# Projecting the first group of heads between the group norms of a two-block transformer kernel

## The chip, the core and the metric

The kernel runs as one program on one core of a Trainium2 chip. The metric is the device time of one execution in microseconds (us), the median of several runs. TensorE (PE) does the matrix products, VectorE (DVE) and ScalarE (ACT) the elementwise work, GpSimd (POOL) some more of it, and SyncE (SP) issues most of the loads. Each engine executes its own list of instructions in a fixed order and waits on semaphores for the others.

## The reference, cut to what matters

Two transformer blocks run one after the other on `x[1, 256, 1024]` in fp32. The change is inside the first block, between its bidirectional RWKV-7 scan and its mixture of experts. For 8 heads of width 64, the two directions of the scan are summed to `y`; then come a group norm per head, a bonus and a gate, and the projection and merge of the two branches:

```python
yn = ((y - mu) * rsqrt(var + GN_EPS)) * ln_g + ln_b          # per head of 64
y_a = (yn + bonus) * g                                        # 256 x 512
merged = sigmoid(gate_a) * (y_a @ proj_a) + sigmoid(gate_b) * (y_b @ proj_b)
x = x + m[2] * (merged @ w_out)                               # then the router and the experts
```

`y_b` is the result of a neighbourhood attention that is done long before. `gate_a` and `gate_b` are 2048 columns of the first input projection `w_in`. The router needs all of the new `x`, so nothing of the experts' work can begin before the last column of `merged @ w_out`.

## The kernel before

Every fp32 product is made of three matmuls in a reduced type (`mm3`, L117 to L121): each operand is a pair of a high and a low part. `split` (L123 to L129) makes such a pair of a 128x512 weight piece: ACT copies the high part (L127) and DVE subtracts it (L128). `prepare` does the same for the large 128x2048 pieces of `w_out` (L180 on ACT, L181 on DVE), and `split_into` for results that are already in PSUM (L940 on ACT, L941 on DVE).

`rwkv` (L876) weaves several generators into one another. Three slots work off the 16 units of the scan (4 chunks of time, 2 directions, 2 groups of four heads). Beside them run `gates` (gate columns of `w_in`, then the products of `proj_b`; their pieces are loaded at L997 and L1015, split by L127/L128, and summed in the PSUM bank "gg"), a generator for the modulation (loads `mr` at L296, worked on by POOL), and `rwkv_out`. `rwkv_out` normalises the sum `y` in four steps `norm(t, g)`: t is a half of the 256 tokens, g a group of four heads. A norm transposes `y` on PE (L898), reduces and squares on DVE and ACT (L903 to L909), takes an inverse square root in some ten small DVE steps (L104 to L115), scales on DVE (L913 to L915), transposes back on PE (L919) and makes the pair `yaT` (L940, L941). The order is group 0, t = 1 and 0, then group 1, t = 1 and 0; each waits until the two units of the scan that it sums are done.

The last unit of the scan ends with L862 to L872 (PE products, with L863, L864, L869 between them), L772 to L784 (PE) and the addition to `y` on DVE (L790). Two units are in hand at once near the end: L828, L834, L837 (PE) with L823 (ACT) and L830 (DVE) belong to the inversion of a triangular matrix in the last one.

After the scan `merge` (L1139) makes `y_a @ proj_a` from eight weight pieces: `product(q, k2)` takes column block q and the head group k2. First the four products of group 0 are issued, then for each q that of group 1, followed by L1173 and L1174 (DVE), L1175 (ACT) and L1176 (DVE), which make the merged pair `mTk`, `mTv`. Then `halves` multiplies by `w_out`, whose four large pieces are split by L180/L181; L1183 and L1184 add the result to the residual. Between them L1737 and L1749 on PE make the router's inputs.

The program's text is not the final order. A scheduler with a cost model reorders the instructions when the kernel is built, subject to the data, the buffers and explicit constraints (`issue_after` keeps an instruction behind another one); after that the order on each engine is fixed. So a norm can stand on DVE between instructions of the scan, and a split of `w_out` between instructions of a norm.

Of the kernel before, what the change touches and what calls it, by code (L numbers as in the profile page):

```python
# [8 lines left out]
F32 = mybir.dt.float32  # L9
# [3 lines left out]
AF = mybir.ActivationFunctionType  # L13
ALU = mybir.AluOpType
# [5 lines left out]
P = 128  # L20
# [51 lines left out]
class Kernel:  # L72
# [803 lines left out]
    def rwkv(self, gates, rest):  # L876
# [5 lines left out]
        turns(gens + [(0, gates), (0, rest), (0, self.rwkv_out(units))])  # L882


    def rwkv_out(self, units):


        nc = self.nc
# [4 lines left out]
        def norm(t, g):  # L893
# [26 lines left out]
            self.split_into(self.yaT[:, 2 * g:2 * g + 2, t * P:(t + 1) * P],  # L920
                            b[:, 0:256].rearrange("p (k t) -> p k t", k=2))
# [66 lines left out]
    def gates(self, pool):  # L988
# [3 lines left out]
        for q in range(8):  # L992
            b = self.bank("gg", 1)
            for k2 in range(4):
# [3 lines left out]
                wt = self.split(pool, raw, [P, 2, 256], "w", bufs=2)  # L998
# [12 lines left out]
        for q in range(4):  # L1011
            b = self.bank("gg", 1)
            for k2 in range(2):
# [3 lines left out]
                wt = self.split(pool, raw, [P, 2, 256], "w", bufs=2)  # L1017
# [6 lines left out]
            nc.vector.scalar_tensor_tensor(g, g, 1.0, b, op0=ALU.add, op1=ALU.mult)  # L1024

# [112 lines left out]

    def merge(self, fp):  # L1139
        nc, a = self.nc, self.a  # L1140
        tt, stt = nc.vector.tensor_tensor, nc.vector.scalar_tensor_tensor
        banks = [self.bank() for _ in range(4)]

        def product(q, k2):

            raw = fp.tile([P, 2, 256], F32, tag="wr", name="wr", bufs=3)
            nc.sync.dma_start(raw, a["proj_a"][0][k2 * 256:(k2 + 1) * 256, 256 * q:256 * q + 256]
                              .rearrange("(k p) n -> p k n", p=P))
            wt = self.split(fp, raw, [P, 2, 256], "w", bufs=2)
            for k in range(2):  # L1150
                for j in range(2):
                    self.mm3(banks[q][:, 256 * j:256 * j + 256], wt[:, k, j * P:(j + 1) * P], self.yaT[:, 2 * k2 + k, :],
                             start=(k2 == k == j == 0), stop=(k2 == 1 and k == 1), skip_group_check=True)
        for q in range(4):
            product(q, 0)
# [40 lines left out]
    def router_inputs(self, pool):  # L1196
        nc = self.nc
# [951 lines left out]
```

## Time and profile before

| | us |
|---|---|
| runs | 1572.23, 1576.36, 1580.75 |
| median | 1576.36 |
| the profiled execution, its own time | 1566.17 |
| its span, from the first to the last instruction | 1564.5 |
| outside the span | 1.7 |
| PE busy in the span | 1457.9 (93%) |

| part of the span | us |
|---|---|
| last addition to `y` (L790) ends | 588.34 |
| last pair `yaT` (L941) ends | 605.83 |
| last column of `merged @ w_out` is taken up (L1183) | 643.40 |

All times in what follows are on the profiled execution's own scale, counted from the start of its span. A row of the timeline reads: start, duration, engine, line and operation, what is written from what, and in brackets how long the engine stood idle before it and what ended that.

### The profile page before, as it was taken

How to read it: one execution, taken by the hardware profiler on the slowest of the kernel's cores; microseconds unless marked ns; L12 is line 12 of the kernel's file. 1: busy time of each engine (PE TensorE's matmuls, PEld its weight loads, DVE VectorE, ACT ScalarE, POOL GpSimd, SP SyncE). 2: the span in 40 equal slices, each digit the busy share in tenths (PEclk: the TensorE clock that was granted, in tenths of full speed). 3: DMA queues.
4: the chain of work that ended last, by engine and by line, in shares of the span. 5: the costliest groups of instructions: out<-in, count | busy, mean ns of one | idle time of the engine just before them, and what ended most of it. 6: DMA issues, size and time to landing. Idle time of an engine off the chain costs nothing.

```text
span 1564.5 us, 26010 instructions
## 1 busy us (share of the span) xinstructions
PE 1457.9 (93%) x10562; PEld 1113.8 (71%) x10562; DVE 889.1 (57%) x1869; ACT 634.8 (41%) x1035; POOL 306.6 (20%) x316
## 2 busy tenths in 40 slices
PE   6899999999999886689999899999999999999996
PEld 3677777778788675543443368699988887998885
DVE  3778458676766676622311255565556755755555
ACT  2433545444454452110110145554444645544443
POOL 1002049765666410490000000000000000000000
PEclk9899999898999897889999999999999999999999
DMA  9511223222232133689999935355554452555542
GB/s 325 162 42 66 68 84 122 79 80 73 69 94 77 56 134 129 258 331 420 421 419 421 380 98 173 108 170 185 186 187 168 155 197 87 183 189 188 188 162 74
DMA packets 118328, 274.21 MB, mean 175 GB/s; under 512 B 8591, under 2 KB 31795, under 8 KB 106935
## 3 DMA queue, kind: packets, MB, share of 16 engines
q1 hardware_dynamic: 115608, 270.13, 49.1%
q10 hardware_dynamic: 2559, 2.32, 0.5%
q8 instruction: 85, 1.39, 0.4%
q14 instruction: 44, 0.36, 0.1%
q0 software_dynamic: 32, 0.00, 0.0%
HBM read 271.36 MB, written 1.06 MB: 174 GB/s over the span
## 4 chain that ended last, share of the span: by engine, by line
PE 54%; DVE 1%; ACT 1%; issue 0%; DVEq 0%; ACTq 0%
PE mm L119 12%; PE mm L120 12%; PE mm L121 12%; PE mm L1476 11%; PE mm L1461 1%; PE mm L1619 1%; PE mm L1540 1%; PE mm L1876 1%; PE mm L1737 1%; PE mm L1895 1%; PE mm L1849 0%; PE mm L1905 0%; PE mm L214 0%; PE mm L1838 0%; DVE wl L181 0%
## 5 line engine op out<-in xcount | busy, mean ns | idle before, releaser
L181 DVE TENSOR_TENSOR wl<-wr,wh 128x2048 fp32r<-128x2048 f32 (+2 forms) x130 | 271.6, 2089 | 208.1 <-ACT wh L180 195.7
L180 ACT ACTIVATE wh<-wr 128x2048 fp32r<-128x2048 f32 (+2 forms) x130 | 227.2, 1749 | 160.7 <-PE mm L121 108.1
L121 PE MATMUL mm<-xTh,wl 128*128 128x256 f32 x512 | 143.9, 281 | 0.0
L120 PE MATMUL mm<-xTl,wh 128*128 128x256 f32 x512 | 143.7, 281 | 0.0
L119 PE MATMUL mm<-xTh,wh 128*128 128x256 f32 x512 | 143.2, 281 | 0.0
L119 PE MATMUL mm<-wh,fh 128*128 128x512 f32 x256 | 101.4, 396 | 0.0
L121 PE MATMUL mm<-wh,fl 128*128 128x512 f32 x256 | 101.1, 395 | 0.0
L120 PE MATMUL mm<-wl,fh 128*128 128x512 f32 x256 | 101.0, 395 | 0.0
L300 POOL TENSOR_SCALAR mr<-mr,silu_c 128x512 f32<-128x512 f32 x56 | 97.8, 1747 | 5.3 <-DMA mr<-in_mod_w_dram 5.1
L120 PEld LDWEIGHTS mm<-xTl,wh 128*128 128x128 f32 x512 | 96.2, 188 | 0.9 <-DVE xTl L941 0.3
L119 PEld LDWEIGHTS mm<-xTh,wh 128*128 128x128 f32 x512 | 96.1, 188 | 0.7
L119 PE MATMUL mm<-wh,xTh 128*128 128x512 f32 (+1 forms) x272 | 95.7, 352 | 0.7 <-ACT big L1813 0.5
L121 PEld LDWEIGHTS mm<-xTh,wl 128*128 128x128 f32 x512 | 96.3, 188 | 0.0
L120 PE MATMUL mm<-wl,xTh 128*128 128x512 f32 (+1 forms) x272 | 93.0, 342 | 0.0
L121 PE MATMUL mm<-wh,xTl 128*128 128x512 f32 (+1 forms) x272 | 92.5, 341 | 0.0
L301 POOL TENSOR_TENSOR mra<-mra,mr 128x512 f32<-128x512 f32 x56 | 74.0, 1322 | 4.2
L823 ACT ACTIVATE nt<-mm 128x512 f16<-128x512 f32 x80 | 47.6, 595 | 59.3 <-PE mm L837 51.8
L119 PEld LDWEIGHTS mm<-wh,xTh 128*128 128x128 f32 x272 | 51.2, 188 | 8.6 <-ACT big L1813 0.7
L121 PEld LDWEIGHTS mm<-wh,fl 128*128 128x128 f32 x256 | 48.1, 188 | 11.5
L120 PEld LDWEIGHTS mm<-wl,fh 128*128 128x128 f32 x256 | 48.1, 188 | 10.7
L119 PEld LDWEIGHTS mm<-wh,fh 128*128 128x128 f32 x256 | 48.1, 188 | 10.6
L121 PEld LDWEIGHTS mm<-wh,xTl 128*128 128x128 f32 x272 | 51.2, 188 | 6.2
(569 smaller groups left out, 3496.4 us busy)
## 6 DMA issues: line engine op xcount, KB each, us to landing
wr<-in_w_up_dram SPq DMA_DIRECT2D x32, 1024.0 KB, 5.6
wr<-in_w_down_dram SPq DMA_DIRECT2D x32, 1024.0 KB, 5.1
wr<-in_w_in_dram SPq DMA_DIRECT2D x22, 1024.0 KB, 5.1
wr<-in_moe_w_dram SPq DMA_DIRECT2D x21, 1024.0 KB, 8.7
wh<-in_moe_w_dram SPq DMA_DIRECT2D x20, 1024.0 KB, 13.8
wl<-in_moe_w_dram SPq DMA_DIRECT2D x20, 1024.0 KB, 12.0
mr<-in_mod_w_dram SPq DMA_DIRECT2D x64, 256.0 KB, 2.8
wx<-in_moe_w_dram SPq DMA_DIRECT2D x14, 1024.0 KB, 10.3
```

The costliest lines, as they stand in the source:

```text
L119: mm(out, l.hi, r.hi, start=start, stop=False, **kw)
L120: mm(out, l.hi, r.lo, start=False, stop=False, **kw)
L121: mm(out, l.lo, r.hi, start=False, stop=stop, **kw)
L180: self.nc.scalar.activation(w.hi, raw, AF.Copy)
L181: self.nc.vector.tensor_tensor(w.lo, raw, w.hi.bitcast(F32), op=ALU.subtract)
L300: nc.gpsimd.tensor_scalar(raw, raw, self.sc[:, k, 0:1], None, op0=ALU.mult)
L301: nc.gpsimd.tensor_tensor(acc, acc, raw, op=ALU.add)
L823: nc.scalar.activation(nt, v4(bz), AF.Copy)
L1461: mm(b[:, k * 256:k * 256 + 256], part[:, t, 2 * q + k, :], sel[:, t].rearrange("p j c -> p (j c)"), start=(i == 0), stop=(i == 3))
L1476: mm(b[r], lT[:, k0 + k, c0 + SLOT * j:c0 + SLOT * j + SLOT], w[:, k], start=(start and k == 0), stop=(stop and k == n - 1))
L1540: mm(acc[2 * n + k // 2][:, k % 2], part[:, k * P:(k + 1) * P], back, start=False, stop=(g == 7 and part is y.lo), skip_group_check=True)
L1619: mm(banks[t], first[:, k, t * P:(t + 1) * P], w[:, k, :], start=(k == 0), stop=False)
```

## The change

1. `rwkv_out` begins only when `gates` has emitted everything ("gates" is added to its first condition and set at the end of `gates`).
2. The products of head group 0 with `proj_a` move out of `merge` and in between the norms: norm(1,0), norm(0,0), three weight pieces, products q = 0 and 1, then product 2 ahead of norm(1,1) and product 3 ahead of norm(0,1). Each product asks for the next weight piece.
3. The split weight pieces of `gates` and of `proj_a` get three buffers instead of two (`bufs=3`).
4. `prepare` of `w_out` is issued behind the last norm's two splitting instructions (`issue_after(self.normed[...])`).
5. The banks are named differently: the router's sums take "gg", `router_inputs` a common bank.

```diff
-        while not {("prep", d, g, i), "bonus"} <= self.past:
+        while not {("prep", d, g, i), "bonus", "gates"} <= self.past:
             yield
+        self.merged = []
         self.yaT = Pair(...)
-        for g in range(2):
-            for t in (1, 0):
-                while not {(0, g, 2 + t), (1, g, 3 - t)} <= self.past:
-                    yield
-                yield from norm(t, g)
+        yield from until((0, 0, 3), (1, 0, 2))
+        yield from norm(1, 0)
+        yield from until((0, 0, 2), (1, 0, 3))
+        yield from norm(0, 0)
+        self.pieces = [self.merge_piece(fp, n) for n in range(3)]
+        for q, tag in enumerate(("gg", "nn1")):
+            self.merge_product(fp, q, 0, tag)
+            yield
+        yield from until((0, 1, 3), (1, 1, 2))
+        self.merge_product(fp, 2, 0, "nn2")
+        yield from norm(1, 1)
+        yield from until((0, 1, 2), (1, 1, 3))
+        self.merge_product(fp, 3, 0, "nn0")
+        yield from norm(0, 1)
...
-                wt = self.split(pool, raw, [P, 2, 256], "w", bufs=2)
+                wt = self.split(pool, raw, [P, 2, 256], "w", bufs=3)
...
+        self.past.add("gates")
...
+    def merge_product(self, fp, q, k2, tag=None):
+        if tag:
+            self.merged.append(self.bank(tag, 1))
+        wt, b = self.pieces.pop(0), self.merged[q]
+        for k in range(2):
+            for j in range(2):
+                self.mm3(b[:, 256 * j:256 * j + 256], wt[:, k, j * P:(j + 1) * P], self.yaT[:, 2 * k2 + k, :],
+                         start=(k2 == k == j == 0), stop=(k2 == 1 and k == 1), skip_group_check=True)
+        n = 4 * k2 + q + 3
+        if n < 8:
+            self.pieces.append(self.merge_piece(fp, n))
...
-        for q in range(4):
-            product(q, 0)
...
         for q in range(4):
-            product(q, 1)
+            self.merge_product(fp, q, 1)
...
-        self.rbank = self.spare()
+        with self.tc.issue_after(self.normed[0]), self.tc.issue_after(self.normed[1]):
+            self.prepare()
+        self.rbank = self.bank("gg", 1)
```

In the changed kernel the lines behind L900 are shifted: the pair `yaT` is made by L921 and L922, the merge's steps are L1196 to L1199, the addition to the residual is L1209 and L1210, the loads of `gates` L1012, its evictions L1020 and L1039.

On DVE, where the scan ends, the rows of before around the last addition to `y` (L790) are these; the small steps are the inverse root of the third norm, and `wl` 128x2048 is a split of `w_out`.

```order
L113 TENSOR_TENSOR rs_t<-rs_u 128x4
L790 TENSOR_TENSOR y_2065<-y_2065,mm 128x256
L114 SCALAR_TENSOR_TENSOR rs_w<-rs_t,va 128x4
L181 TENSOR_TENSOR wl<-wr,wh 128x2048
L115 SCALAR_TENSOR_TENSOR rs_u<-rs_w,rs_u 128x4
L181 TENSOR_TENSOR wl<-wr,wh 128x2048
L113 TENSOR_TENSOR rs_t<-rs_u 128x4
L114 SCALAR_TENSOR_TENSOR rs_w<-rs_t,va 128x4
L115 SCALAR_TENSOR_TENSOR grs<-rs_w,rs_u 128x4
L913 TENSOR_TENSOR yn<-yn,grs 128x256
L181 TENSOR_TENSOR wl<-wr,wh 128x2048
```

In the changed kernel the same place on DVE reads as follows, from the last unit's L864 to the first norm, norm(1,0).

```order
L864 TENSOR_TENSOR rr_7223<-rr_7223,mm 128x512
L128 TENSOR_TENSOR wl<-wr,wh 128x512
L869 TENSOR_TENSOR rq_7476<-rr_7223,mm 128x512
L1039 SCALAR_TENSOR_TENSOR gt<-gt,mm 128x512
L128 TENSOR_TENSOR wl<-wr,wh 128x512
L774 TENSOR_TENSOR z_7887<-mm,krT_7226 128x256
L790 TENSOR_TENSOR y_2065<-y_2065,mm 128x256
L903 TENSOR_REDUCE mu<-mm 128x4
L904 TENSOR_SCALAR mu<-mu 128x4
L905 TENSOR_TENSOR yn<-mm,mu 128x256
```

All four norms now stand behind the last addition to `y`; before, the first two and the beginning of the third stood ahead of it, and three splits of `w_out` stood inside the third.

Further down DVE's list, inside the third norm, norm(1,1), the changed kernel has splits of `proj_a` pieces (`wl` 128x512).

```order
L114 SCALAR_TENSOR_TENSOR rs_w<-rs_t,va 128x4
L128 TENSOR_TENSOR wl<-wr,wh 128x512
L115 SCALAR_TENSOR_TENSOR grs<-rs_w,rs_u 128x4
L913 TENSOR_TENSOR yn<-yn,grs 128x256
L914 TENSOR_TENSOR yn<-yn,gf 128x256
L128 TENSOR_TENSOR wl<-wr,wh 128x512
L915 TENSOR_TENSOR yn<-yn,gf 128x256
L128 TENSOR_TENSOR wl<-wr,wh 128x512
L922 TENSOR_TENSOR yaTa<-mm,yaTw 128x2x128
```

Three of its four splits stand ahead of L915, the norm's last scaling, and the fourth stands ahead of the pair `yaT` (L922).

On PE, the last unit's products of before stand behind the transposes (L919) of the second norm.

```order
L1200 MATMUL mm<-rw,fac 128x16 x8
L919 MATMUL mm<-ident,yn 128x128 x2
L868 MATMUL mm<-z_7913,mk_7392 128x128 x4
L898 MATMUL mm<-ident,y_2066 128x128 x2
L872 MATMUL mm<-rq_7476,tT_2093 128x128 x4
L772 MATMUL mm<-mk_7392,rr_7223 64x128 x4
L781 MATMUL mm<-mk_7392,zv 64x128 x2
```

In the changed kernel L868, the last ten matmuls of `gates` and L872 follow each other (just ahead of these rows), and the first norm's transposes come behind the unit's last product; the 48 matmuls of head group 0 (with `yaTw`, `yaTa`) begin behind the third norm's first transposes.

```order
L772 MATMUL mm<-mk_7392,rr_7223 64x128 x4
L781 MATMUL mm<-mk_7392,zv 64x128 x2
L781 MATMUL mm<-mk_7392,rr_7223 64x128 x2
L781 MATMUL mm<-mk_7392,zv 64x128 x2
L781 MATMUL mm<-mk_7392,rr_7223 64x128 x2
L784 MATMUL mm<-z_7887,sbd_2092 128x128 x2
L898 MATMUL mm<-ident,y_2066 128x128 x2
L919 MATMUL mm<-ident,yn 128x128 x2
L898 MATMUL mm<-ident,y_2065 128x128 x2
L919 MATMUL mm<-ident,yn 128x128 x2
L898 MATMUL mm<-ident,y_2066 128x128 x2
L119 MATMUL mm<-yaTw,wh 128x256 x3
```

So PE no longer waits for a norm inside the scan, and the products of group 0 fall between the second and the third norm's transposes back.

On DVE behind the last pair `yaT`, before, the merge's steps come in one run and the last split of `w_out` (L181) at its end.

```order
L1176 TENSOR_TENSOR mTv<-mu_8201,mTk 128x512
L1174 TENSOR_TENSOR mu_8224<-mu_8224,gt 128x512
L1173 SCALAR_TENSOR_TENSOR mu_8247<-gt,mm 128x512
L1176 TENSOR_TENSOR mTv<-mu_8224,mTk 128x512
L1174 TENSOR_TENSOR mu_8247<-mu_8247,gt 128x512
L1173 SCALAR_TENSOR_TENSOR mu_8270<-gt,mm 128x512
L1176 TENSOR_TENSOR mTv<-mu_8247,mTk 128x512
L1174 TENSOR_TENSOR mu_8270<-mu_8270,gt 128x512
L1176 TENSOR_TENSOR mTv<-mu_8270,mTk 128x512
L181 TENSOR_TENSOR wl<-wr,wh 128x2048
```

The changed kernel has there, from the last norm's end (L922) on, the four splits of `w_out` between the merge's steps L1196, L1197 and L1199.

```order
L922 TENSOR_TENSOR yaTa<-mm,yaTw 128x2x128
L181 TENSOR_TENSOR wl<-wr,wh 128x2048
L1196 SCALAR_TENSOR_TENSOR mu_8219<-gt,mm 128x512
L128 TENSOR_TENSOR wl<-wr,wh 128x512
L1197 TENSOR_TENSOR mu_8219<-mu_8219,gt 128x512
L1196 SCALAR_TENSOR_TENSOR mu_8236<-gt,mm 128x512
L181 TENSOR_TENSOR wl<-wr,wh 128x2048
L1199 TENSOR_TENSOR mTv<-mu_8219,mTk 128x512
L1197 TENSOR_TENSOR mu_8236<-mu_8236,gt 128x512
L1196 SCALAR_TENSOR_TENSOR mu_8253<-gt,mm 128x512
L181 TENSOR_TENSOR wl<-wr,wh 128x2048
L1199 TENSOR_TENSOR mTv<-mu_8236,mTk 128x512
```

Three of the four splits have moved from the third norm to here, ahead of the third and the fourth `mTv`.

At the start of the scan, on ACT, the order of before is this: two weight splits of `gates`, then a unit's L680 and the next unit's L652.

```order
L127 ACTIVATE wh<-wr 128x512 x2
L680 ACTIVATE z_2137<-mm 128x256
L652 ACTIVATE th<-mm 128x512
L738 ACTIVATE rr_2133<-mm 128x256
L823 ACTIVATE nt_2253<-mm 128x512
```

The changed kernel has one split more ahead of L652.

```order
L127 ACTIVATE wh<-wr 128x512 x2
L680 ACTIVATE z_2137<-mm 128x256
L127 ACTIVATE wh<-wr 128x512
L652 ACTIVATE th<-mm 128x512
L738 ACTIVATE rr_2133<-mm 128x256
```

The fifth piece of `gates` is split ahead of the unit's L652, and likewise the seventh ahead of a later L680; the third buffer of point 3 allows it.

## Rows read from the trace of the kernel before

**Rows 1.** Windows: stretch, length, busy time by engine, granted clock, DMA share and GB/s

```profile
588.00:606.00 18.00, 2.79 (x12) 2.45 (x13) 14.11 (x33) 3.08 (x5) 0.00 (x0) 0.58 0.68 234
...
618.00:643.40 25.40, 25.29 (x123) 20.57 (x123) 13.75 (x28) 5.94 (x10) 0.00 (x0) 1.00 0.46 162
```

The engines in these rows are PE, PEld (PE's weight loads), DVE, ACT and POOL, each with its busy time and its number of instructions.

**Rows 2.** Timeline of DVE, where the scan ends and in the norms

```profile
568.40 0.42 DVE L790 TENSOR_TENSOR y<-y,mm 128x256 f32<-128x256 f32 x1
...
579.29 0.42 DVE L915 TENSOR_TENSOR yn<-yn,gf 128x256 f32<-128x256 f32 x1
...
587.92 0.42 DVE L790 TENSOR_TENSOR y<-y,mm 128x256 f32<-128x256 f32 x1 [0.91 <-PE mm L784]
...
598.41 0.41 DVE L903 TENSOR_REDUCE mu<-mm 128x4 f32<-128x256 f32 x1
...
605.41 0.42 DVE L941 TENSOR_TENSOR yaTa<-mm,yaTw 128x256 fp32r<-128x256 f32 x1 [1.26 <-ACT yaTw L940]
```

**Rows 3.** Timeline of PE, where the scan ends

```profile
561.67 1.12 PE L868 MATMUL mm<-z,mk 128*128 128x128 f32 x8
...
569.64 0.31 PE L828 MATMUL mm<-nt,a 64*64 64x64 f16 x8
...
579.77 0.44 PE L919 MATMUL mm<-ident,yn 128*128 128x128 f32 x2 [1.02 <-DVE yn L915]
580.04 1.35 PE L868 MATMUL mm<-z,mk 128*128 128x128 f32 x8
...
596.96 0.66 PE L919 MATMUL mm<-ident,yn 128*128 128x128 f32 x2 [9.07 <-DVE yn L915]
```

**Rows 4.** Timeline of ACT, two results of the last unit that PE needs

```profile
566.80 0.60 ACT L823 ACTIVATE nt<-mm 128x512 f16<-128x512 f32 x1 [1.57 <-PE mm L837]
...
574.52 0.60 ACT L863 ACTIVATE z<-mm 128x512 f32<-128x512 f32 x1
```

**Rows 5.** Groups, 588 to 606: count, busy time, mean ns, idle before

```profile
L181 DVE TENSOR_TENSOR wl<-wr,wh 128x2048 fp32r<-128x2048 f32 x3 | 6.8, 2283 | 0.0
```

**Rows 6.** Timeline of PE: first and 48th product with proj_a, second and 48th with w_out

```profile
604.61 0.56 PE L119 MATMUL mm<-yaTw,wh 128*128 128x256 f32 x1
...
611.81 0.28 PE L121 MATMUL mm<-yaTw,wl 128*128 128x256 f32 x1
...
618.07 0.41 PE L120 MATMUL mm<-wl,mTk 128*128 128x512 f32 x1
...
628.81 0.40 PE L121 MATMUL mm<-wh,mTv 128*128 128x512 f32 x1
```

**Rows 7.** Timelines of DVE and ACT in the merge

```profile
614.83 0.68 DVE L1174 TENSOR_TENSOR mu<-mu,gt 128x512 f32<-128x512 f32 x1
615.43 0.68 DVE L1173 SCALAR_TENSOR_TENSOR mu<-gt,mm 128x512 f32<-128x512 f32 x1
...
622.61 0.69 DVE L1176 TENSOR_TENSOR mTv<-mu,mTk 128x512 fp32r<-128x512 f32 x1 [0.70 <-ACT mTk L1175]
...
643.40 0.69 DVE L1183 TENSOR_TENSOR mo<-mm,m2row 128x512 f32<-128x512 f32 x1 [1.93 <-PE mm L121]
...
623.65 1.92 ACT L180 ACTIVATE wh<-wr 128x2048 fp32r<-128x2048 f32 x1 [1.07 <-PE mm L121]
```

**Rows 8.** Timelines of ACT and SP, at the start of the scan

```profile
232.54 0.60 ACT L652 ACTIVATE th<-mm 128x512 f32<-128x512 f32 x1 [3.41 <-PE mm L650]
...
240.88 0.38 ACT L680 ACTIVATE z<-mm 128x256 f32<-128x256 f32 x1 [0.56 <-PE mm L679]
...
227.96 3.91 SPq L296 DMA_DIRECT2D mr<-in_mod_w_dram  x2
231.97 0.38 SPq L997 DMA_DIRECT2D wr<-in_w_in_dram  x1
...
241.86 0.39 SPq L997 DMA_DIRECT2D wr<-in_w_in_dram  x1
```

**Rows 9.** Line L997, 225 to 250: how long its loads took

```profile
DMA to landing us min/median/max: 3.0/3.3/3.6
```

More of the change, by code (lines that the diff above doesn't have):

```diff
@@ L874, in solve, with rwkv @@
         yield
-    def rwkv(self, gates, rest):
+    def rwkv(self, gates, rest, fp):
         units = [(i, d, g) for i in range(4) for d, g in ((0, 0), (1, 0), (0, 1), (1, 1))]
@@ L880, in rwkv, with rwkv_out @@
         gens = [(s * LEAD, self.rwkv_slot(s, units[s::SLOTS], state, self.y)) for s in range(SLOTS)]
-        turns(gens + [(0, gates), (0, rest), (0, self.rwkv_out(units))])
-    def rwkv_out(self, units):
+        turns(gens + [(0, gates), (0, rest), (0, self.rwkv_out(units, fp))])
+    def rwkv_out(self, units, fp):
         nc = self.nc
@@ L919, in norm, with until @@
                 nc.tensor.transpose(b[:, p * P:(p + 1) * P], y[:, p * P:(p + 1) * P], self.ident)
[L920 to L921 removed]
+            dst, b = self.yaT[:, 2 * g:2 * g + 2, t * P:(t + 1) * P], b[:, 0:256].rearrange("p (k t) -> p k t", k=2)
+            self.normed = [nc.scalar.activation(dst.hi, b, AF.Copy).ins,
+                           tt(dst.lo, b, dst.hi.bitcast(F32), op=ALU.subtract).ins]
             yield
         i, d, g = units[-1]
[L924 removed]
+        while not {("prep", d, g, i), "bonus", "gates"} <= self.past:
             yield
+        self.merged = []
         self.yaT = Pair(*(self.zp.tile([P, 4, 256], F32R, tag=f"tl{n}", name=f"yaT{n}") for n in "wa"))
[L927 to L932 removed]
+        def until(*units):
+            while not set(units) <= self.past:
+                yield
[6 more added lines that the diff above has]
+            self.merge_product(fp, q, 0, tag)
+            yield
+        yield from until((0, 1, 3), (1, 1, 2))
[4 more added lines that the diff above has]
+        yield from norm(0, 1)
     def spare(self):
@@ L1016, in gates @@
                                   .rearrange("(k p) n -> p k n", p=P))
-                wt = self.split(pool, raw, [P, 2, 256], "w", bufs=2)
+                wt = self.split(pool, raw, [P, 2, 256], "w", bufs=3)
                 for k in range(2):
@@ L1136, in na, with merge_piece @@
             yield
+    def merge_piece(self, fp, n):
+        q, k2 = n % 4, n // 4
+        raw = fp.tile([P, 2, 256], F32, tag="wr", name="wr", bufs=3)
+        self.nc.sync.dma_start(raw, self.a["proj_a"][0][k2 * 256:(k2 + 1) * 256, 256 * q:256 * q + 256]
+                               .rearrange("(k p) n -> p k n", p=P))
+        return self.split(fp, raw, [P, 2, 256], "w", bufs=3)
+    def merge_product(self, fp, q, k2, tag=None):
[9 more added lines that the diff above has]
+            self.pieces.append(self.merge_piece(fp, n))
     def merge(self, fp):
@@ L1141, in merge @@
         tt, stt = nc.vector.tensor_tensor, nc.vector.scalar_tensor_tensor
[L1142 to L1153, printed above, removed]
-        for q in range(4):
-            product(q, 0)
         mT = Pair(*(self.zp.tile([P, 8, 256], F32R, tag=f"z{i}", name=f"mT{i}") for i in "kv"))
@@ L1197, in router_inputs @@
         nc = self.nc
-        b = self.spare()
+        b = self.bank()
         for k in range(8):
@@ L2096, in body @@
             k.rwkv_params()
-            k.rwkv(k.gates(fp), k.factors(fb, hp))
+            k.rwkv(k.gates(fp), k.factors(fb, hp), fp)
             for t in range(2):
```

2 lines of the change are left out of this document (1 added, 1 removed).

## The prediction

> **What bounds the kernel now.** I read the windows first, to find the stretch in which TensorE does not work, then the timelines of DVE, PE and ACT there. In the scan and in the product with `w_out` PE is the bound: from 618 to 643.4 it is busy for 25.29 of 25.4 us [rows 1]. In between, from 588 to 606, it is busy for 2.79 of 18 us, and DVE for 14.11 [rows 1]. This is the stretch of the norms. The reader should see two waits in PE's rows: 9.07 us for the third norm's L915, and 1.02 us for the second norm's, with the scan's own L868 queued behind it [rows 3]. Of the four norms only two lie in the open. The last addition to `y` ends at 588.34 [rows 2]; by then DVE has finished the first two norms beside the scan. From there to the end of the last pair `yaT`, 605.41 + 0.42 = 605.83 [rows 2], are 17.5 us. In them lie three splits of `w_out`, 6.8 us [rows 5], in the middle of the third norm. I call the end of that pair T0. From T0 to the last L1183 at 643.40 [rows 7] are 37.6 us. Behind it the router and the experts need everything, so what is lost or won up to there stays.
>
> **The change, part by part.** I follow the path in four terms.
>
> *First term, the start of the scan.* The third weight buffer lets a fifth piece be split ahead of the unit's L652 at 232.54 and a seventh ahead of L680 at 240.88 [rows 8]. Both ACT steps now wait for loads. The fifth load is issued at 231.97 behind seven `mr` loads, the seventh at 241.86 behind ten [rows 8]; in the new order of SP they stand behind six and nine. An `mr` load takes about 3.91/2 = 2.0 us [rows 8], so the seventh load would be issued at about 239.5, land 3.3 later [rows 9], and after its split of 0.6 ACT would be free near 243.4, some 2.5 us behind 240.88. DVE's subtraction for the fifth piece adds 0.7 ahead of the other slots' work. Part of it is made up, since PE has other slots. I take **+2.0**, with bounds of 0 (all covered) and +3.5.
>
> *Second term, the end of the scan.* The norms of group 0 leave the scan's interior. L828 at 569.64 stood behind a norm's transposes; its input, L823, was ready at 566.80 + 0.60 = 567.40 [rows 3, 4], and PE had other products until about 568.1, so 1.5 us go. L868 at 580.04 stood behind the second norm's transposes at 579.77, which waited for DVE's L915 at 579.29 [rows 2, 3]. Its own input, L863, was ready at 575.12 [rows 4]; less the 1.5 that is 573.6. From L868 to the addition took 568.40 − 561.67 = 6.7 us in the unit before, and 587.92 − 580.04 = 7.9 in the last one [rows 2, 3]. I take the shorter, because PE has the last matmuls of `gates` between, and get 573.7 + 6.7 = 580.4 against 587.92: **−7.5**. Bounds: −6.4 with 7.9 us, −9.5 if the waits ahead of L863 go too.
>
> *Third term, from the last addition to the last pair.* All four norms now follow the last addition on DVE, one behind the other; what was done beside the scan is done in the open. The last norm of before shows the price undisturbed: from its L903 at 598.41 to the pair's end at 605.83 are 7.42 us [rows 2], and the next norm could begin 0.08 earlier, since DVE's steps overlap a little. So three norms at 7.34 and one at 7.42 make 29.4. Three of the four `proj_a` splits inside the third norm stand in its chain, at 0.69 each (the size of L1176 [rows 7]): 2.1, with bounds 0 and 2.8. Sum 31.5 in place of 17.5: **+14.0**. Put otherwise: two norms in the open +14.7, three splits of `w_out` out −6.8 [rows 5], small splits in +2.1, and the rest is what overlapped in the third norm. The 48 products of group 0 on PE (7.2 us, from 604.61 to 611.81 [rows 6]) are hidden under the norms; if that cover failed they would cost up to 7.2 as before.
>
> *Fourth term, from T0 to the last L1183.* PE has 7.2 us less to do. But the splits of `w_out` that left the third norm now stand between the merge's steps on DVE. Its list after T0: a wait of 1.5 until ACT's first L180 (1.92 [rows 7]) is through, four splits at 2.2 (2.28 [rows 5], less the overlap), one split and twelve merge steps at 0.60 each (614.83 to 615.43 [rows 7]): 1.5 + 8.8 + 7.8 = 18.1. The fourth split waits in addition for its slot: as before, the last L180 waits for PE to finish with the first piece [rows 7], and here this needs the second `mTv`, at about T0 + 12.9; 12 matmuls at 0.233 ((628.81 − 618.07)/46 [rows 6]), a copy of 1.92 and a split of 2.2 put it at T0 + 19.8 and the last `mTv` at T0 + 20.5. Before, that step ended at 622.61 + 0.69 = 623.30, T0 + 17.5 [rows 7]. Of the 96 matmuls, 60 need it or come behind those that do: 60 × 0.233 = 14.0. The products for the router between them take 3.2 (25.3 [rows 1] less 96 × 0.233). So 20.5 + 14.0 + 3.2 = 37.7 against 37.6: **0**. Bounds: −5.8, were PE the limit (7.2 less, and 1.4 for the router's sums and the transposes that now stand there), and +7, were half of the product with `w_out` done at the lower clock.
>
> The sum: 2.0 − 7.5 + 14.0 + 0 = **+8.5 us**. From the profiled execution, 1566.2, that is 1574.7. Its runs' median, 1576.36, lies 10 us above this execution; on it the forecast is **1585**, +0.54%.
>
> [...]
>
> **The rivals.**
>
> *PE sets the pace after T0.* If DVE's splits slide under the products (the first of them could run while PE transposes the last norm), the last `mTv` comes before PE needs it, and the fourth term is −5.8: +2.7, 1579. It decides at T0 + 14.5 or so for the last `mTv`. Against it: four splits alone are 8.8 us on DVE, and the fourth must wait for its slot.
>
> *The clock stays low.* PE works in small groups up to T0 + 20.5, with longer gaps than before. If the matmuls of 14 us behind this start at the lower level and half of them pass at it, 7 us come on top: +15.5, about 1591. For it speaks the clock of 0.58 in the norms [rows 1]; against it that before, too, the first products with `proj_a` ran behind such a stretch and the clock was back by 618.
>
> *Interleaving pays.* The change could do what its words say: group 0's products hidden under the norms, −7.2, and the splits out of the norm, −6.8, while the first two norms stay beside the scan: −14.0, 1562, **faster**. It is decided by whether the norms of group 0 run before the last addition; in the order of the changed kernel DVE has all four behind it, so I give it little. [...]
>
> **How the numbers follow.** Forecast (+8.5, its own range +4 to +13: 1580 to 1589): 0.50. PE sets the pace (+2.7, 1576 to 1582): 0.22. Low clock (+15.5, up to 1595): 0.15. Interleaving pays: 0.08. The rest, small shifts in the scan around 0: 0.05. The range leaves out the interleaving and the far end of the low clock: 1576 to 1593. About 0.5%, 7.9 us, is what a measurement of this kernel can tell from no change, and +8.5 lies just above it. Slower: 0.30 of the forecast's 0.50, the low clock's 0.15 and 0.02 of PE's pace, 0.47. Faster: 0.07. Same: 0.46.
>
> **What would show it.** In the changed profile: the last L790 near 582.5 (580.4 and the 2 of the start); behind it four norms, their L903 some 7.3 apart, 9.4 at the third; the last `yaT` near 614; PE's wait for L915 no longer inside the scan, and the 48 products of group 0 between the second and the third norm's transposes back; the last `mTv` 20.5 behind the last `yaT`, and the last L1209 at about 652. If a norm's L903 comes before the last L790, the second and third terms are wrong; if PE is busy without a gap from T0 on, the fourth is; if the granted clock is under 1.00 from the last `mTv` on, the second rival holds. A large shift at L652 near 232 would make the first term wrong.

## The result and the profile after

Over 20 runs of either kernel the medians are 1585.84 us after and 1571.58 us before; the ratio is 1.0095, 95% interval 1.0075 to 1.0114. The change makes the kernel slower by about 15 us. The forecast was slower by 8.5, so its direction holds and its size is short. The before median of this comparison lies 5 us under that of the three runs which the prediction had; that the forecast of 1585 falls beside the measured 1585.84 is luck, a start 5 us too high and a change 6 us too small. What is compared from here on is the ratio. The profiled execution of the changed kernel spans 1576.5 us, 12.0 more than that of before.

```profile
span 1576.5 us, 26014 instructions
...
PE 1461.1 (93%) x10562; PEld 1114.5 (71%) x10562; DVE 884.8 (56%) x1869; ACT 633.8 (40%) x1035; POOL 307.5 (20%) x316
```

The page's first lines give away nothing: the busy times are those of before within 5 us. The timeline of DVE is where the change shows. The rows answer to [rows 2] and [rows 7]; behind start and duration stand engine, line, operation, what is written from what, and the idle time before it with its end.

```profile
581.65 0.42 DVE L790 TENSOR_TENSOR y<-y,mm 128x256 f32<-128x256 f32 x1 [1.08 <-PE mm L784]
581.99 0.42 DVE L903 TENSOR_REDUCE mu<-mm 128x4 f32<-128x256 f32 x1
...
589.40 0.41 DVE L903 TENSOR_REDUCE mu<-mm 128x4 f32<-128x256 f32 x1
...
596.82 0.42 DVE L903 TENSOR_REDUCE mu<-mm 128x4 f32<-128x256 f32 x1
...
606.16 0.41 DVE L903 TENSOR_REDUCE mu<-mm 128x4 f32<-128x256 f32 x1
...
613.16 0.42 DVE L922 TENSOR_TENSOR yaTa<-mm,yaTw 128x256 fp32r<-128x256 f32 x1 [1.26 <-ACT yaTw L921]
614.96 2.29 DVE L181 TENSOR_TENSOR wl<-wr,wh 128x2048 fp32r<-128x2048 f32 x1 [1.37 <-ACT wh L180]
618.93 0.69 DVE L1196 SCALAR_TENSOR_TENSOR mu<-gt,mm 128x512 f32<-128x512 f32 x1 [1.68 <-PE mm L121]
...
632.86 2.29 DVE L181 TENSOR_TENSOR wl<-wr,wh 128x2048 fp32r<-128x2048 f32 x1 [1.62 <-ACT wh L180]
635.07 0.68 DVE L1199 TENSOR_TENSOR mTv<-mu,mTk 128x512 fp32r<-128x512 f32 x1
...
652.65 0.69 DVE L1209 TENSOR_TENSOR mo<-mm,m2row 128x512 f32<-128x512 f32 x1 [1.93 <-PE mm L121]
```

The last addition (L790) comes first, then four norms, 7.41, 7.42 and 9.34 us apart and the last one 7.42 long, up to 613.58. Then come the large splits, with waits among them: 1.37 and 1.62 us for ACT, and 1.68 us for PE. The last `mTv` ends 22.2 us behind the last `yaT`, not 20.5, and the last L1209 follows 39.1 behind it, not 37.7.

PE's rows, answering to [rows 3] and [rows 6]:

```profile
570.67 0.31 PE L828 MATMUL mm<-nt,a 64*64 64x64 f16 x8
...
576.03 1.16 PE L868 MATMUL mm<-z,mk 128*128 128x128 f32 x8
...
612.05 0.66 PE L919 MATMUL mm<-ident,yn 128*128 128x128 f32 x2 [6.46 <-DVE yn L915]
612.50 3.43 PE L1226 MATMUL mm<-rw,fac 128*128 128x16 f32 x16
615.77 0.78 PE L119 MATMUL mm<-yaTw,wh 128*128 128x256 f32 x2
```

L868 waits for no norm any more. But eight matmuls for the router, L1226 (16 records of them), stand between the last norm and the first product of group 1, and take 3.4 us. Before, the same eight (L1200) ran at 576.79, in a gap of PE, in 2.0 us.

The windows, stage by stage, answer to [rows 1]: the norms; the first 5.3 us of the products of group 1; up to the start of the second half of the merge; the rest.

```profile
582.10:613.60 31.50, 12.05 (x68) 10.93 (x69) 22.41 (x84) 6.20 (x13) 0.00 (x0) 0.68 0.37 131
613.60:618.90 5.30, 5.30 (x25) 5.30 (x26) 2.29 (x1) 3.45 (x4) 0.00 (x0) 0.50 0.14 8
618.90:634.00 15.10, 14.17 (x74) 11.85 (x74) 13.02 (x15) 6.52 (x7) 0.00 (x0) 0.94 0.62 207
634.00:652.60 18.60, 16.76 (x85) 13.39 (x84) 8.82 (x21) 2.17 (x6) 0.00 (x0) 1.00 0.61 217
```

The granted clock is 0.50 in the second window, just behind a norm in which PE waited 6.46 us, 0.94 in the third and 1.00 from 634 on.

At the start of the scan, ACT's rows and the load that one of them waits for, answering to [rows 8]:

```profile
234.47 0.63 ACT L127 ACTIVATE wh<-wr 128x512 fp32r<-128x512 f32 x1 [3.58 <-DMA wr<-in_w_in_dram]
235.01 0.58 ACT L652 ACTIVATE th<-mm 128x512 f32<-128x512 f32 x1
...
246.18 0.63 ACT L127 ACTIVATE wh<-wr 128x512 fp32r<-128x512 f32 x1 [4.59 <-DMA wr<-in_w_in_dram]
246.72 0.58 ACT L1020 ACTIVATE gt<-mm 128x512 f32<-128x512 f32 x1
247.20 0.38 ACT L680 ACTIVATE z<-mm 128x256 f32<-128x256 f32 x1
...
242.56 0.39 SPq L1012 DMA_DIRECT2D wr<-in_w_in_dram  x1
```

In this execution the scan's first L662 starts 2.5 us later than in that of before (224.57 against 222.09). In the eight kernels of the next table with two buffers, whose code up to there is the same, this place lies anywhere from 222 to 229, so I take the 2.5 as scatter. Less these 2.5, the fifth split holds nothing up (L652 at 232.5, as before), but the seventh waits 4.59 us for its load, and L680 behind it is 3.8 us later than the 240.88 of [rows 8].

To compare kernels I cut each profiled execution at the same six places: PE's first L662 (start of the scan), its first L306 (a matmul of the modulation, some 28 us later), its last L354 (an instruction ahead of the scan's end that is the same in all), the end of the last addition to `y`, the end of the last `yaT`, the start of the last addition to the residual, L1183 or what it is called there. All kernels of the experiments are in it; times in us.

| kernel | scan, to L306 | scan, to L354 | scan's end | norms | merge |
|---|---|---|---|---|---|
| before | 27.7 | 307.2 | 31.3 | 17.5 | 37.6 |
| after | 35.2 | 299.6 | 22.7 | 31.5 | 39.1 |
| gate_wait_only | 27.6 | 297.6 | 24.3 | 36.9 | 38.0 |
| no_gate_wait | 34.5 | 303.6 | 33.8 | 13.8 | 39.0 |
| no_gate_no_hold | 33.3 | 310.6 | 32.7 | 21.6 | 36.3 |
| hold_only | 27.6 | 306.9 | 31.2 | 10.7 | 43.2 |
| w3_only | 33.3 | 302.1 | 31.9 | 17.5 | 38.4 |
| after_w2 | 27.6 | 307.2 | 22.7 | 31.4 | 39.5 |
| after_no_rsh | 33.3 | 308.5 | 22.7 | 31.2 | 36.9 |
| pool_split | 27.6 | 299.0 | 38.2 | 15.2 | 37.7 |
| nogate_w2_pool | 27.6 | 306.6 | 32.7 | 29.0 | 35.8 |
| hold_each | 27.6 | 297.4 | 31.3 | 11.5 | 40.8 |
| hold_late | 27.6 | 297.6 | 28.5 | 13.6 | 40.7 |

The last three columns repeat within some tenths of a us where the code of the stage is the same (scan's end: before, hold_only and hold_each; scan's end and norms: after, after_w2 and after_no_rsh; merge: hold_each and hold_late), and so does the first with two buffers (27.6 seven times). With three buffers the first is 33.3 three times, 34.5 and 35.2 for the same instructions, to which the section on the prediction comes back. The second column does not repeat: it scatters by 10 us, which has a section of its own at the end. So the tail of the kernel is read from one profile each, and the scan from the timings.

### The profile page after: what moved, and what is told of

Read it like the earlier page. It is cut to its first block, busy times and chain, and to the rows that moved or that the text cites. A ratio compares the mean times of both kernels' runs of the same rounds, so it can differ in the third digit from the quotient of the medians.

```text
span 1576.5 us, 26014 instructions
## 1 busy us (share of the span) xinstructions
PE 1461.1 (93%) x10562; PEld 1114.5 (71%) x10562; DVE 884.8 (56%) x1869; ACT 633.8 (40%) x1035; POOL 307.5 (20%) x316
## 4 chain that ended last, share of the span: by engine, by line
PE 54%; DVE 1%; ACT 1%; issue 0%; DVEq 0%; ACTq 0%
PE mm L119 12%; PE mm L120 12%; PE mm L121 12%; PE mm L1502 11%; PE mm L1487 1%; PE mm L1566 1%; PE mm L1645 1%; PE mm L1902 1%; PE mm L1763 1%; PE mm L1921 1%; PE mm L1875 0%; PE mm L1931 0%; PE mm L214 0%; PE mm L1864 0%; DVE wl L181 0%
## 5 line engine op out<-in xcount | busy, mean ns | idle before, releaser
L181 DVE TENSOR_TENSOR wl<-wr,wh 128x2048 fp32r<-128x2048 f32 (+2 forms) x130 | 271.6, 2090 | 209.8 <-ACT wh L180 197.4
L823 ACT ACTIVATE nt<-mm 128x512 f16<-128x512 f32 x80 | 47.6, 595 | 62.9 <-PE mm L837 55.1
L121 PEld LDWEIGHTS mm<-wh,fl 128*128 128x128 f32 x256 | 48.1, 188 | 11.5
L120 PEld LDWEIGHTS mm<-wl,fh 128*128 128x128 f32 x256 | 48.1, 188 | 10.7
```

Of the source, the lines that this page charges most:

```text
L120: mm(out, l.hi, r.lo, start=False, stop=False, **kw)
L121: mm(out, l.lo, r.hi, start=False, stop=stop, **kw)
L181: self.nc.vector.tensor_tensor(w.lo, raw, w.hi.bitcast(F32), op=ALU.subtract)
L823: nc.scalar.activation(nt, v4(bz), AF.Copy)
```

## The experiments

Theory: the loss is the norms of group 0 in the open (third term, +14), of which the scan's end gives 7.5 back; the merge is even. Rivals: the splits of `w_out` behind the norms are the loss; the third weight buffer is; or the difference is scatter.

**gate_wait_only**: the kernel before, with the one condition.

```diff
-        while not {("prep", d, g, i), "bonus"} <= self.past:
+        while not {("prep", d, g, i), "bonus", "gates"} <= self.past:
```

> The kernel before with one thing of the change: the norms wait until the gate products have all been emitted, which puts all four norms behind the scan's last addition on VectorE. Theory (the exposed norms are the loss): the last addition comes 7 to 9 us earlier than in the kernel before, the stretch from there to the last pair yaT grows from 17.5 to about 36 us (four norms of 7.3 and three splits of w_out of 2.2 in the first of them), the merge stays at 37.6; in sum about +10 us, ratio 1.006. Rival (the splits of w_out behind the norms are the loss): no difference beyond 0.3%.

Measured 1.0064 (1.0036 to 1.0093). The scan's end is 7.0 us shorter, the norms are 36.9, the merge 38.0: +12.8 in the three. The condition alone takes the norms apart from the scan and costs what the theory says.

**no_gate_wait**: the changed kernel without the condition (the diff above, reversed).

> The changed kernel without that one wait; the products of head group 0 between the norms and the splits of w_out behind the norms stay. Theory: the last addition as in the kernel before, about 588; the third norm loses 6.6 us of w_out splits and gains 1.4 to 2.8 of small ones, so the last yaT comes 2 to 5 us earlier than before; the merge takes 39 as in the changed kernel; in sum -1 to -4 us, ratio about 0.998. Rival (the splits behind the norms are the loss): still 1.005 to 1.01.

Measured 1.0070 (1.0034 to 1.0105): slower than before, although its last three stages sum to 86.6 us against 86.4. So something outside of them costs, and it is not the splits either: the scan to L306 takes 34.5 us, as in the changed kernel. Within the tail the theory is off, too: the norms are 3.7 shorter, as expected, but the scan's end is 2.4 longer. PE's rows show why:

```profile
580.65 0.69 PE L919 MATMUL mm<-ident,yn 128*128 128x128 f32 x2 [4.37 <-DVE yn L915]
581.13 1.91 PE L868 MATMUL mm<-z,mk 128*128 128x128 f32 x8
582.69 0.56 PE L119 MATMUL mm<-yaTw,wh 128*128 128x256 f32 x1
...
583.91 1.03 PE L872 MATMUL mm<-rq,tT 128*128 128x128 f32 x4
```

L868 has waited for the norm for 4.37 us, takes 1.91 us in place of the 1.35 of [rows 3] (the granted clock is 0.78 from 581 to 592.6), and the first products of group 0 then stand between it and L872, and more of them ahead of L772. Products that were to fill a gap lie in the scan's own chain.

**no_gate_no_hold**: the same, and the splits of `w_out` not kept behind the norms.

```diff
-        with self.tc.issue_after(self.normed[0]), self.tc.issue_after(self.normed[1]):
-            self.prepare()
```

> The changed kernel without the wait and without the order that keeps the splits of w_out behind the norms: three of the splits then stand in the fourth norm. Theory: the last yaT about 2 us later than in the kernel before, the merge shorter by the 48 products of group 0, 5 to 6 us, since TensorE and not VectorE sets its pace; in sum -3 to -4 us, ratio 0.9975. Rival (hidden products give nothing back): 1.001.

Measured 1.0052 (1.0027 to 1.0078). The norms grow to 21.6 (three large splits and three small ones in their chain), and the merge falls by 1.3 to 36.3 only. So 48 products fewer behind the norms are worth 1.3 us, not 7.2: the eight router matmuls come in their place, and the low clock, which the first products ran through before, now falls on those of group 1. A row of PE and a window behind the last `yaT` show both:

```profile
619.24 3.44 PE L1224 MATMUL mm<-rw,fac 128*128 128x16 f32 x16
```

```profile
620.33:628.50 8.17, 8.17 (x39) 8.17 (x40) 2.37 (x4) 1.44 (x3) 0.00 (x0) 0.50 0.06 26
```

PE has no gap there, and the granted clock is 0.50 for 8.2 us; before, it was 0.66 from 605.83 to 609 and 1.00 behind that.

**hold_only**: the kernel before, and only the splits kept behind the norms (the two lines of the diff above added, and `normed` recorded for them).

> The kernel before with the splits of w_out kept behind the last norm and nothing else of the change. Theory: the last yaT 6.6 us earlier, the merge 6 to 8 us longer, because two large splits stand ahead of the small ones that the products of group 0 wait for; in sum 0 to +1.5 us, ratio 1.000. Rival (the splits behind the norms are the loss of the change): +8 to +14 us, 1.005 to 1.009.

Measured 0.9979 (0.9955 to 1.0003): no loss. The norms are 6.8 shorter, the merge 5.6 longer. The rival falls.

**w3_only**: the kernel before, with the third buffer at each of the three places that ask for it; one is shown.

```diff
-                wt = self.split(pool, raw, [P, 2, 256], "w", bufs=2)
+                wt = self.split(pool, raw, [P, 2, 256], "w", bufs=3)
```

> The kernel before with the third buffer for the split weights of the gates and nothing else. Theory (the first term was too small: the third buffer makes the scan's start wait for loads and costs the scan 6 to 9 us): +6 to +9 us, ratio 1.004 to 1.006; the gates' first eviction on ScalarE (L1005) comes 3 to 7 us later than in the kernel before against the start of the scan, and the last addition to y some 5 us later. Rival (the first term as predicted, +2, made up later): 1.000 to 1.002. Second rival (the scan's length only scatters): no shift of the first eviction either.

Measured 1.0050 (1.0019 to 1.0081), about +8 us, by a change that only lets a split go earlier. The scan to L306 takes 33.3 us in place of 27.7. ACT's rows:

```profile
238.07 0.63 ACT L127 ACTIVATE wh<-wr 128x512 fp32r<-128x512 f32 x1 [4.46 <-DMA wr<-in_w_in_dram]
238.61 0.58 ACT L652 ACTIVATE th<-mm 128x512 f32<-128x512 f32 x1
...
245.51 0.63 ACT L127 ACTIVATE wh<-wr 128x512 fp32r<-128x512 f32 x1 [0.66 <-PE mm L120]
246.57 0.38 ACT L680 ACTIVATE krT<-mm 128x256 f32<-128x256 f32 x1 [0.44 <-PE mm L679]
```

The fifth split waits 4.46 us for its load and L652 stands behind it. The eight kernels with two buffers take 27.6 or 27.7 us to L306, the five with three 33.3 to 35.2; in this case there is no overlap. That it is the wait of ACT for loads which stretches the scan's start is read from these rows; moving the loads ahead instead was not tried. What the clock adds to it is told with the first term below.

**after_w2**: the changed kernel with two buffers, everything behind the scan left as it is.

```diff
-                wt = self.split(pool, raw, [P, 2, 256], "w", bufs=3)
+                wt = self.split(pool, raw, [P, 2, 256], "w", bufs=2)
...
-        self.pieces = [self.merge_piece(fp, n) for n in range(3)]
+        self.pieces = [self.merge_piece(fp, n) for n in range(2)]
...
-        n = 4 * k2 + q + 3
+        n = 4 * k2 + q + 2
```

> The changed kernel with two buffers for the split weights instead of three (and two pieces of proj_a asked for ahead instead of three); the norms, the products between them and the splits behind them stay. Theory (third buffer costs 6 to 9 us, norms and merge the rest): about +7 us against the kernel before, ratio 1.004 to 1.006, below the changed kernel's 1.0095. Rival (the third buffer costs nothing in the end): 1.009 to 1.010. The stretch from the last addition to the last pair yaT stays at 31.5 us in both.

Measured 1.0026 (0.9994 to 1.0058), and the norms 31.4. Its tail is 7.3 us longer than that of before, which the interval (-1 to +9 us) holds. Against the changed kernel's 1.0095 the third buffer is worth some 11 us, with a wide margin, beside the 8 that w3_only shows. Beside gate_wait_only, which has the same condition, the tail is 5.5 us shorter (93.6 against 99.1): so much the products between the norms and the splits behind them give back together.

**after_no_rsh**: the changed kernel without the router's eight matmuls; the constant part of the router's sums is left out, so other experts are chosen.

```diff
-        b = self.bank()
-        for k in range(8):
-            nc.tensor.matmul(b[:, 0:16], self.fac[:, 16 + k:17 + k].to_broadcast([P, P]), self.rw[:, k, :],
-                             start=(k == 0), stop=(k == 7))
         self.rsh = pool.tile([P, 16], F32, name="rsh")
-        nc.scalar.activation(self.rsh, b[:, 0:16], AF.Copy)
+        nc.vector.memset(self.rsh, 0.0)
```

> The changed kernel with the eight small matmuls of the router's constant part left out and zero in their place, so the router's choice is another. Theory (these eight, 3.4 us at the lower clock behind the last norm, are why VectorE waits for TensorE in the merge of the changed kernel): from the last yaT to the last L1209 37.0 to 37.6 us instead of 39.0. Rival (the first products wait for the lower clock anyway): 38.5 to 39. Its total time is not compared, since another choice of experts may change the loop over them.

Its total time is not compared, since other experts run. Its merge takes 36.9 us, 2.2 less than the changed kernel's. DVE's rows:

```profile
625.13 0.42 DVE L922 TENSOR_TENSOR yaTa<-mm,yaTw 128x256 fp32r<-128x256 f32 x1 [1.26 <-ACT yaTw L921]
626.93 2.29 DVE L181 TENSOR_TENSOR wl<-wr,wh 128x2048 fp32r<-128x2048 f32 x1 [1.37 <-ACT wh L180]
629.13 0.68 DVE L1196 SCALAR_TENSOR_TENSOR mu<-gt,mm 128x512 f32<-128x512 f32 x1
```

The wait of 1.68 us ahead of the first L1196 is gone. So PE's router matmuls, not DVE's list alone, set the start of the merge.

**pool_split**: the kernel before, with the first three low parts of `w_out` on GpSimd, where nothing runs in the norms. It asks whether DVE's list is what bounds the norms, and was a try at a faster kernel.

```diff
-            self.nc.vector.tensor_tensor(w.lo, raw, w.hi.bitcast(F32), op=ALU.subtract)
+            self.npre = getattr(self, "npre", 0) + ("w_out" in key[0] and "2" not in key[0])
+            lo = self.nc.gpsimd if "w_out" in key[0] and "2" not in key[0] and self.npre <= 3 else self.nc.vector
+            lo.tensor_tensor(w.lo, raw, w.hi.bitcast(F32), op=ALU.subtract)
```

> The kernel before with the low parts of the first three splits of w_out on GpSimd, which does nothing between 580 and 643 us, instead of VectorE. Theory (VectorE's list is what bounds the norms): the third norm loses 6 to 7 us, the merge is unchanged at 37.6, in sum -6 us, ratio 0.996. [...] One of the 128x2048 instructions should take 4 to 6 us there, four times the 1.3 of the 128x512 ones.

Measured 1.0019 (0.9984 to 1.0053), not the theory's 0.996. The three stages sum to 91.1 us, 4.7 more than before. Rows of POOL and DVE:

```profile
576.78 4.51 POOL L183 TENSOR_TENSOR wl<-wr,wh 128x2048 fp32r<-128x2048 f32 x1 [22.07 <-ACT wh L180]
...
576.94 4.38 DVE L906 TENSOR_SCALAR mu<-mu 128x4 f32<-128x4 f32 x1
...
584.10 4.49 POOL L183 TENSOR_TENSOR wl<-wr,wh 128x2048 fp32r<-128x2048 f32 x1 [2.81 <-ACT wh L180]
...
584.12 4.50 DVE L113 TENSOR_TENSOR rs_t<-rs_u 128x4 f32<-128x4 f32 x1
```

A step of DVE on 128x4 elements, 0.16 or 0.17 us elsewhere, takes 4.4 or 4.5 and ends with the GpSimd instruction beside it. These steps of DVE stand still for its length, which is twice the 2.28 that the same split takes on DVE [rows 5].

**nogate_w2_pool**: what is left of the change with the condition, the third buffer and the order of the splits taken away, and the first three low parts on GpSimd.

> The changed kernel without the wait for the gates, without the third buffer and without the order that keeps the splits of w_out behind the norms; their low parts go to GpSimd instead. What stays of the change is the 48 products between the norms. Theory: the last yaT some 4 us earlier than in the kernel before (three large splits out, three small ones in), the merge 1 to 3 us shorter; in sum -5 to -7 us, ratio 0.996. Rival (the hidden products give nothing, as the router's eight small matmuls and the products of group 1 then run at the lower clock behind the last norm): the merge stays at 37 to 39 and the sum is -2 to -4, ratio 0.998.

Measured 1.0064 (1.0031 to 1.0096). The merge falls to 35.8, but the norms take 29.0, as three GpSimd instructions stand in the fourth norm from 606.35 on for 13.4 us, and DVE with them. It says nothing on the products that no_gate_no_hold did not say.

**hold_each**: the kernel before, each low part held where DVE is idle: the first behind the last norm's pair (`self.normed`), the next two behind the last step of an `mT`.

```diff
...
-            self.nc.vector.tensor_tensor(w.lo, raw, w.hi.bitcast(F32), op=ALU.subtract)
+            with self.tc.issue_after(self.held.pop(0)) if getattr(self, "held", None) else nullcontext():
+                self.nc.vector.tensor_tensor(w.lo, raw, w.hi.bitcast(F32), op=ALU.subtract)
...
-            tt(fl(mT.lo[:, js, :]), u, fl(mT.hi[:, js, :].bitcast(F32)), op=ALU.subtract)
+            last = tt(fl(mT.lo[:, js, :]), u, fl(mT.hi[:, js, :].bitcast(F32)), op=ALU.subtract).ins
+        self.held = [self.normed[1], last, last]
...
```

> The kernel before with the low parts of the first three splits of w_out put behind other instructions on VectorE one by one: the first behind the last pair yaT, where VectorE is idle for 2.2 us, the second and third behind the last mTv, where it is idle again. Theory (what the change's splits cost in the merge is that they stand ahead of mTv, and what they cost in the norms is 2.2 each): the last yaT 6 to 7 us earlier than in the kernel before, the merge 1 to 3 us longer, in sum -4 to -6 us, ratio 0.997. Rival (TensorE's product with w_out then waits for the second and third split at each piece): the merge 6 us longer and the sum near 0.

Measured 0.9977 (0.9950 to 1.0004). The norms are 6.0 shorter, the merge 3.2 longer: -2.8 us in the profile, a little less than expected, and within what the timing allows. It beats the changed kernel; that it beats the kernel before is likely and not shown.

**hold_late**: hold_each, and the second norm's first scaling behind the last unit's L869.

```diff
...
-        tt(rq, rr, br.rearrange("p (h a n) -> p a h n", h=4, a=2), op=ALU.add)
+        self.rq = tt(rq, rr, br.rearrange("p (h a n) -> p a h n", h=4, a=2), op=ALU.add).ins
+        self.nrq = getattr(self, "nrq", 0) + 1
...
-            tt(h3(y), h3(y), b3(rs, 4), op=ALU.mult)
+            while (t, g) == (0, 0) and getattr(self, "nrq", 0) < 16:
+                yield
+            with self.tc.issue_after(self.rq) if (t, g) == (0, 0) else nullcontext():
+                tt(h3(y), h3(y), b3(rs, 4), op=ALU.mult)
...
```

> hold_each, and the second norm's scalings (with its transposes back) held behind the last unit's L869 on VectorE, so that TensorE's L868 no longer waits for that norm. Theory (what the changed kernel won at the end of the scan, 8.6 us, came from L868 and L828 not waiting for norms, and 4 to 5 of it can be had without putting the norms behind the scan): from the last L354 to the end of the last addition 26 to 28 us instead of 31.3, the norms 11.5 to 12.5, the merge 40.8 as in hold_each; in sum -6 to -7 us against the kernel before, ratio 0.996. Rival (the second norm then ends so late that the third waits for it): the norms 14 us or more and the sum as in hold_each, -3.

Measured 1.0000 (0.9969 to 1.0031). The scan's end is 2.8 us shorter, the norms 2.0 longer, since the third norm now begins later beside the scan. Between theory and rival, nearer to the rival: taken together -0.8 us against hold_each, which no timing here can show.

## Why the prediction was right, and where not

**The bound** was read rightly. The norms are DVE's chain; gate_wait_only, which changes nothing but their place, costs 10 us.

**Second term** (scan's end, -7.5, bounds -6.4 to -9.5): measured -8.6 (31.3 to 22.7). L868 is free of the norm, as put: counted from L354 it starts 6.3 us earlier, as forecast (580.04 to 573.7). From there to the start of the addition it took 5.6 us (576.03 to 581.65), under the 6.7 that I took; from 576 to 582 the granted clock was 1.00, where before it was 0.59 from 580.04 to 588.34.

**Third term** (+14.0): measured 31.52 against 17.50, +14.0. The cycle of 7.34 was 7.41 and 7.42, the third norm with its splits 9.34 in place of 9.4. This term carried the forecast and was taken from one undisturbed norm of the trace of before.

**Fourth term** (0): measured +1.5, inside its bounds. The last `mTv` came at 22.2, not 20.5. The step that failed is PE's share: I counted 1.4 us for the router's sums and the transposes in the lower bound and nothing in the list that I took. The eight router matmuls took 3.4 us at a granted clock of 0.50 (612.5 to 615.9) and made DVE wait for 1.68; after_no_rsh gives them 2.2 of the merge. The rival that PE sets the pace after T0 would have been 5.8 shorter; no_gate_no_hold, where DVE does not hold it up, shows 1.3. So its price was too high: 48 products moved away did not take 7.2 with them, because what follows runs through the low clock instead (0.50 for 8.2 us). One figure of this term was slightly off by its own formula: 25.3 less 96 × 0.233 is 2.9 for the router's products, not 3.2. The +7 of the upper bound and the 7 us of the rival of a clock that stays low both count with half of the full clock, which the rows that they rest on (0.58 and 1.00) do not show; behind T0 the changed kernel ran at 0.50 for 5.3 us only, from 613.6 on. That rival did not come: the clock was 0.94 from 618.9 and 1.00 from 634 on. Nor did interleaving pay: no norm's L903 came before the last L790.

**First term** (+2.0, bounds 0 to +3.5): this is the term that was mis-sized. I worked out 2.5 us for one wait, of the seventh load, and took part of it as made up. To L306 the scan lost 7.5 us in the changed kernel and 5.6 in w3_only, and the timing of w3_only gives about 8 in the end (3 to 13). The load itself was put rightly (issued at 242.56, 240.1 without the shift of 2.5; forecast at 239.5, where 241.86 less one `mr` load of 2.0 is 239.9); the split began 3.6 us after the issue, and L680, with an eviction (L1020) between it and the split, lost 3.8 us rather than 2.5. L652 did not shift, so the sign that I had named for this term stayed out although the term was too small. What I missed stands in PE's rows, of after and then of before:

```profile
247.63 0.80 PE L728 MATMUL mm<-krT,z 64*128 64x128 f32 x4 [2.70 <-ACT z L680]
...
248.71 1.44 PE L728 MATMUL mm<-krT,z 64*128 64x128 f32 x8
...
251.26 1.54 PE L737 MATMUL mm<-zv,mk 128*128 128x64 f32 x6
```

```profile
242.04 1.01 PE L728 MATMUL mm<-krT,z 64*128 64x128 f32 x8
...
243.72 0.88 PE L737 MATMUL mm<-zv,mk 128*128 128x64 f32 x6
```

I counted on the other slots to fill PE's gap. But ACT's steps for all slots stand in one list behind the waiting split; PE stands idle for 2.70 us for L680, and its next matmuls then take up to 1.75 times as long (1.54 against 0.88, 1.44 against 1.01). ACT's L823 behind them waits 3.38 us for PE at 251.44, where the same step of before waits 2.14 at 243.89. So 3.8 us on L680 have become 7.5 at L306. The windows from the first L662 to the first L306, of before, after and w3_only in turn, show how (the granted clock is the third number from the right):

```profile
222.09:249.79 27.70, 25.34 (x266) 20.35 (x266) 25.05 (x45) 13.90 (x31) 25.74 (x18) 1.00 0.47 143
```

```profile
224.57:259.80 35.23, 29.58 (x267) 23.48 (x266) 21.38 (x46) 14.19 (x32) 27.55 (x24) 0.81 0.37 116
```

```profile
227.30:260.58 33.28, 28.77 (x266) 23.33 (x266) 25.46 (x46) 14.40 (x32) 26.83 (x24) 0.85 0.39 121
```

PE works off the same 266 matmuls (one record more or less). Its idle time grows from 2.4 us to 5.7 in the changed kernel, 3.3 more, and its busy time from 25.3 to 29.6, 4.2 more: PE waited, the granted clock was 0.50 from 245.3 to 259.0, and the same matmuls took longer. More than half of the 7.5 is this clock, for which my term held nothing; in w3_only it is 3.4 of 5.6. The mean granted clock of this stretch is 1.00 in all eight kernels with two buffers and 0.81 to 0.85 in all five with three.

**The sum**: -8.6 + 14.0 + 1.5 is +6.9 in the profile, and 8 of the third buffer make 15, the measured ratio's 15. The forecast's 8.5 is 6 short of it: the first term is 6 too small, and the errors of the second (−1.1) and the fourth (+1.5) nearly cancel. The profiled executions alone would have hidden it: their scans (first two columns) are 334.9 and 334.8 us long, because that of before holds stretches at a lower clock (0.90 from 260 to 400) which the other lacks. Beside scans that lack them too the loss is there: pool_split, hold_each and hold_late, with two buffers and a granted clock of 1.00 from 260 to 400 like the changed kernel's, take 326.6, 325.0 and 325.2 us for it, 8 to 10 less than its 334.8. For the same reason it is luck that the last addition ended at 582.07, near the 582.5 that I had named. What the 0.4 to 0.9 us of the merge in w3_only and after_w2 against before and after come from, and the up to 4 us by which the part behind the merge differs between executions, stays open.

## What to carry to other kernels

The deeper buffer let a split go ahead in ACT's queue; its load was not there yet, everything behind it on ACT waited (4.59 us in the changed kernel), and TensorE, left without work, lost more by the lower clock (4.2 us of busy time, at a mean granted clock of 0.81) than by the wait itself (3.3 us). So before adding a buffer look at when the loads land and not only at when the buffer comes free. Work that a scheduler has woven into another stage is free only there: a condition added for order's sake, here that the gates be done, can take it out, and its price can be read from one undisturbed repetition of it. The 48 products that were moved out from behind a low clock did not take their measured 7.2 us with them but 1.3; the work behind them ran at 0.50 for 8.2 us instead (no_gate_no_hold).

## What the runs showed of the hardware

**VectorE stood still beside GpSimd.** While GpSimd ran a 128x2048 subtraction between buffers in SBUF (4.5 us), a DVE step on 128x4 took 4.38 and 4.50 us in place of 0.16, once a TENSOR_SCALAR and once a TENSOR_TENSOR, and ended together with it. In the third such meeting of pool_split a TENSOR_REDUCE that began 0.26 us behind the GpSimd instruction took its usual 0.42 us, and the TENSOR_SCALAR after it 3.81, up to that instruction's end. In all three the stop lasts to the end of the GpSimd instruction (4.49 to 4.51 us), though the step stopped has only 128x4 elements. What holds VectorE there the rows do not show.

**The scan's length scatters by 10 us with the same code.** The second column of the table is near 297 to 299 or near 307 us for kernels whose instructions up to there are the same. The windows from 330 to 370 us show it, of the kernel before, hold_only, gate_wait_only and hold_each in turn (the granted clock is the third number from the right):

```profile
330.00:370.00 40.00, 37.33 (x388) 31.35 (x388) 27.55 (x54) 16.68 (x36) 25.14 (x22) 0.83 0.26 80
```

```profile
330.00:370.00 40.00, 37.06 (x378) 31.26 (x378) 27.53 (x54) 15.98 (x35) 27.12 (x23) 0.79 0.26 80
```

```profile
330.00:370.00 40.00, 37.12 (x478) 31.57 (x477) 29.53 (x64) 20.31 (x47) 29.92 (x26) 1.00 0.26 81
```

```profile
330.00:370.00 40.00, 36.89 (x475) 31.09 (x474) 29.56 (x66) 20.01 (x44) 29.93 (x26) 1.00 0.26 82
```

PE is busy for 37 of 40 us in all four, but at a clock of 0.83 or 0.79 it has 378 to 388 of its records instead of 475 or more. A drop of the clock somewhere in the scan comes in some executions and not in others. The scatter is larger than any term of this change but the norms', and one profile of each kernel cannot tell a loss of 8 us in the scan from it unless the clock of the stretch is read beside it. The part ahead of the scan scatters too (its end lies between 222 and 229 us in the kernels with two buffers); how the two share the spread of 20 us in the runs of one kernel, and what sets the drops off, stays open.
